# FFN input product in a fixed order on DVE and ACT, its weights one block ahead, its stores on POOL's queue

## The chip, the cores and the metric

The kernel runs on one core of a Trainium2 chip. The metric is device time in microseconds (us), the median of several runs. TensorE (PE) multiplies, VectorE (DVE), ScalarE (ACT) and GpSimd (POOL) work on tiles, SyncE (SP) and POOL issue transfers (DMA). Each engine has one queue of instructions and works through it in order; an instruction waits until what it reads is there, and holds all that stand behind it on its engine.

## The reference, cut to what matters

```python
for layer in range(2):                      # T = 1024 tokens, D_MODEL = 1024, D_FF = 2816
    hn = rmsnorm(h, norm_gains[layer, 0])
    mixed = fox_attention(hn, ...) if layer % 2 == 0 else hgrn2_recurrence(hn, ...)
    h = h + rmsnorm(mixed, norm_gains[layer, 1])
    hn = rmsnorm(h, norm_gains[layer, 2])
    h = h + rmsnorm(swiglu_ffn(hn, ffn_w_in[layer], ffn_w_out[layer]), norm_gains[layer, 3])

def swiglu_ffn(h, w_in, w_out):
    gate, up = jnp.split(jnp.einsum('bsd,df->bsf', h, w_in), 2, axis=-1)
    return jnp.einsum('bsf,fd->bsd', jax.nn.silu(gate) * up, w_out)
```

All of it is fp32.

## The kernel before

An fp32 product is three matmuls of a rounded type: each operand is split in a high part (a cast on ACT, L178) and a low part (a subtraction on DVE, L181), and hi·hi, hi·lo and lo·hi are summed in PSUM. `split` does both; the tiles are whi and wlo for weights, p1h and p1l to p7h and p7l for x.

The FFN input product multiplies 2 × 2 quadrants with seven products in place of eight: the quadrants of w_in (a11, a12, a21, a22) and of x (r11, r12, r21, r22) are first added and subtracted, then seven products p1 to p7 of 12 matmuls of 128 x 512 are made, then added into the results. `ffn_in` loops over 22 blocks of weight columns, gate and up in turn. From the fifth block on the order of products on PE is p1, p5, p4 of the block before, p2, p6, p3, p7. For the first four blocks p1 and p2 are computed ahead, from x operands that are ready early (`ffn_ahead`; `first` keeps copies of their p1).

`operands` loads a block's weights (wl, the two lower quadrants, L407; wst, the upper ones, L411, both on SP), forms the sums (L401) and splits them. It is called within the block, and the order in which DVE takes the sums, lo parts and results (`gate`, `up`: silu on ACT at L452, product with the up half at L459) is left to a scheduler that works from simulated times. Only the casts are chained among themselves (`queue`).

Of x, `Quadrants.put` writes a token tile's transposed columns (psx is their PSUM tile) into raw tiles; `Quadrants.sums` makes the sums for p5, p6, p3, p7 and p4 in two parts of 256 columns (four token tiles each). Both are called after the last tile of the mixer's output product. The last tile comes to it through `boundary`, which adds the mixer's output to h (`postnorm`, with rs from POOL), stores h (L333, SP), normalises it (`prenorm`, L281) and transposes it.

`out_sums` runs beside `ffn_in`: it loads rows of w_out (wrow, L538, SP), makes four sums of them (tsum, L544 to L548) and stores these (tw0a, tw0b, tw1a, tw1b, POOL's queue, L546, L549) for the FFN output product. The results of `ffn_in` go to DRAM as aT (L461, SP). `ffn_out` reads aT and tw back through ring tiles as and ws (L576, L597, SP), splits them, and hands its results (cx, cy, cu, cv; L628) to `boundary`, which in layer 2 stores the output out (L333, SP).

`hgrn_consts` makes the masks and bounds (lm, tb; L1005 to L1036) of the recurrence of layer 2; it is called after layer 1's `ffn_in`.

The lines that set pools and order:

```python
BUFS = dict(s=3, g=3, l=2, ws=2)
self.wst = pool("wst", 3)
with self.tc.issue_after(self.casts[queue].ins) if queue in self.casts else nullcontext():
```

Of the kernel before, what the change touches and what calls it, by code (L numbers as in the profile page):

```python
# [7 lines left out]
F32 = mybir.dt.float32  # L8
F32R = mybir.dt.float32r
# [41 lines left out]
BUFS = dict(s=3, g=3, l=2, ws=2)  # L51
# [7 lines left out]
DPOS = (1,)  # L59

# [13 lines left out]
class Quadrants:  # L74
# [9 lines left out]
    def __init__(self, pool, work):  # L84
        self.op, self.raw, self.work = {}, {}, work
        for n, tag in enumerate(self.PLACES):
            self.raw[self.NAMES[n % 4], n // 4] = work.tile([P, 4, 256], F32, name=self.NAMES[n % 4], tag=tag, bufs=BUFS[tag])
        self.take(pool, self.EARLY)
# [5 lines left out]
    def put(self, trunk, b, tt, ps):  # L94
# [3 lines left out]
        raw = self.raw[f"r{b + 1}{t + 1}", p // 2][:, :, p % 2 * P:(p % 2 + 1) * P]  # L98
# [5 lines left out]
    def sums(self, trunk, part):  # L104

        V = trunk.nc.vector
        r11, r22, r12, r21 = (self.raw[n, part] for n in self.NAMES)
        cs = slice(part * 256, (part + 1) * 256)
        split = lambda m, t, ks=slice(0, 4): trunk.split(*(x[:, ks, cs] for x in self.op[m]), t)
        n = 4 if part else 2  # L110
        for k in range(0, 4, n):
            ks = slice(k, k + n)
            if part:
                t = trunk.nrm.tile([P, n, 256], F32, name="rsum", tag="u", bufs=trunk.nb[1])
            else:
                t = self.work.tile([P, n, 256], F32, name="rsum", tag="ws", bufs=BUFS["ws"])
            V.tensor_tensor(out=t, in0=r12[:, ks], in1=r11[:, ks], op=ALU.subtract)
            split("p5", t, ks)
        V.tensor_tensor(out=r12, in0=r22, in1=r12, op=ALU.subtract)
        V.tensor_tensor(out=r11, in0=r12, in1=r11, op=ALU.add)  # L120
        split("p6", r11)
        split("p3", r22)
        split("p7", r12)
        V.tensor_tensor(out=r21, in0=r21, in1=r11, op=ALU.subtract)
        split("p4", r21)

class Trunk:
    def __init__(self, ctx, tc, a):
# [6 lines left out]
        self.sums_of, self.casts = {}, {}  # L135
        self.const = pool("const")
        self.wst = pool("wst", 3)
# [37 lines left out]
    def split(self, hi, lo, src, lo_engine=None, queue=None):  # L175

        with self.tc.issue_after(self.casts[queue].ins) if queue in self.casts else nullcontext():
            cast = self.nc.scalar.copy(out=hi, in_=src)  # L178
        if queue is not None:
            self.casts[queue] = cast  # L180
        (lo_engine or self.nc.vector).tensor_tensor(out=lo, in0=src, in1=hi.bitcast(F32), op=ALU.subtract)  # L181

    def unit(self, srcs, shape, keep=None):

        nc = self.nc
        with self.tc.high_priority(offset=self.ahead):
            st = self.wst.tile([P] + shape, F32, name="wst", tag="wst")
            for dst, src in srcs:
                nc.sync.dma_start(out=dst(st), in_=src)
# [86 lines left out]
    def prenorm(self, h, gB, xT, tt, keep=True, step=1):  # L276

        nc = self.nc
        rs = self.squares((h,))
# [1170 lines left out]
```

## Time and profile before

| | us |
|---|---|
| median of 3 runs (lowest, highest) | 2590.56 (2587.06, 2591.43) |
| profiled execution, its own time | 2588.12 |
| span of its profile | 2586.3 |
| PE busy | 2486.8 (96%) |
| FFN input product, layer 1 (638.12 to 1094.02) | 455.9, of which PE busy 438.4 |
| FFN input product, layer 2 (1894.73 to 2352.22) | 457.5, of which PE busy 439.3 |

The stages in order are: first norm, attention with its projections (to about 583), the attention's output product (to 638), FFN input and output of layer 1 (to about 1390), HGRN2 and its output product (to 1894), FFN of layer 2. The profile gives busy time of each engine in any stretch, a timeline with the idle time in front of an instruction and what ended it (in brackets), and a table of waits. PE's granted clock is 1.00 where it runs at its upper level.

### The profile page before, as it was taken

How to read it: one execution, taken by the hardware profiler on the slowest of the kernel's cores; microseconds unless marked ns; L12 is line 12 of the kernel's file. 1: busy time of each engine (PE TensorE's matmuls, PEld its weight loads, DVE VectorE, ACT ScalarE, POOL GpSimd, SP SyncE). 2: the span in 40 equal slices, each digit the busy share in tenths (PEclk: the TensorE clock that was granted, in tenths of full speed). 3: DMA queues.
4: the chain of work that ended last, by engine and by line, in shares of the span. 5: the costliest groups of instructions: out<-in, count | busy, mean ns of one | idle time of the engine just before them, and what ended most of it. 6: DMA issues, size and time to landing. Idle time of an engine off the chain costs nothing. (4 is left out here: it accounts for less than half of the span.)

```text
span 2586.3 us, 35183 instructions
## 1 busy us (share of the span) xinstructions
PE 2486.8 (96%) x12616; PEld 2079.6 (80%) x12616; DVE 1664.0 (64%) x2875; ACT 1105.0 (43%) x2128; POOL 432.7 (17%) x654
## 2 busy tenths in 40 slices
PE   6999999999898999999999999999999989999997
PEld 6898989878676888788879988887877778887885
DVE  5767676767766455476866585766575654455675
ACT  5556565655433333354542222223452333334443
POOL 4434343422000000000231111114200100000022
PEclk9999999999999999999999999999999999999998
DMA  4211111225478222384641211114534852226554
GB/s 123 47 34 37 41 35 34 62 86 169 115 227 265 87 73 83 93 297 135 220 135 38 74 46 55 48 58 139 175 107 155 275 169 84 78 70 226 185 181 166
DMA packets 302127, 305.43 MB, mean 118 GB/s; under 512 B 54648, under 2 KB 229752, under 8 KB 301952
## 3 DMA queue, kind: packets, MB, share of 16 engines
q1 hardware_dynamic: 292736, 275.91, 34.5%
q0 software_dynamic: 9216, 27.27, 3.2%
q8 instruction: 99, 1.62, 0.3%
q14 instruction: 76, 0.62, 0.1%
HBM read 228.67 MB, written 74.45 MB: 117 GB/s over the span
## 5 line engine op out<-in xcount | busy, mean ns | idle before, releaser
L157 PE MATMUL op<-whi,a 128*128 128x512 f32 x1232 | 384.4, 392 | 15.0 <-DVE cx L628 7.5
L178 ACT CAST whi<-wst 128x512 fp32r<-128x512 f32 x288 | 177.3, 619 | 410.7 <-PE m L157 201.7
L157 PEld LDWEIGHTS op<-whi,a 128*128 128x128 f32 x1232 | 232.2, 189 | 67.4 <-issue 8.3
L181 DVE TENSOR_TENSOR wlo<-wst,whi 128x512 fp32r<-128x512 f32 x240 | 168.2, 704 | 134.7 <-ACT whi L178 134.4
L157 PE MATMUL op<-wlo,a 128*128 128x512 f32 x616 | 241.0, 391 | 0.8 <-DVE wlo L181 0.8
L157 PE MATMUL pv<-whi,xTh 128*128 128x256 f32 x512 | 150.0, 293 | 4.4 <-DVE k L771 4.4
L157 PE MATMUL pv<-wlo,xTh 128*128 128x256 f32 x512 | 145.8, 285 | 0.0
L157 PE MATMUL pv<-whi,xTl 128*128 128x256 f32 x512 | 145.5, 284 | 0.0
L157 PEld LDWEIGHTS op<-wlo,a 128*128 128x128 f32 x616 | 116.2, 189 | 25.2 <-DVE wlo L181 1.4
L796 ACT ACTIVATE p<-p,mn 128x128 f32<-128x128 f32 (+7 forms) x128 | 99.2, 776 | 78.5 <-DVE mn L795 77.6
L181 DVE TENSOR_TENSOR pl<-pT,ph 128x512 fp32r<-128x512 f32 (+1 forms) x160 | 100.8, 633 | 47.5 <-ACT ph L178 44.5
L181 DVE TENSOR_TENSOR wlo<-wl,whi 128x512 fp32r<-128x512 f32 x88 | 60.4, 688 | 99.7 <-ACT whi L178 99.7
L795 DVE CUSTOM_DVE_ANT_0 p<-s,mask 128x128 f32<-128x128 f32 (+7 forms) x128 | 93.1, 755 | 37.3 <-PE s L157 36.5
L181 DVE TENSOR_TENSOR wlo<-ws,whi 128x512 fp32r<-128x512 f32 x154 | 104.9, 684 | 10.9 <-ACT whi L178 10.5
L157 PE MATMUL pqk<-xTh,whi 128*128 128x512 f32 x256 | 110.1, 430 | 0.0
L178 ACT CAST ph<-pT 128x512 fp32r<-128x512 f32 (+1 forms) x160 | 86.7, 544 | 50.7 <-PE pT L161 48.1
L178 ACT CAST whi<-ws 128x512 fp32r<-128x512 f32 x154 | 95.2, 619 | 22.3 <-DMA ws<-in_ffn_w_out_dram 7.6
L157 PEld LDWEIGHTS pv<-whi,xTh 128*128 128x128 f32 x512 | 97.9, 191 | 5.1 <-issue 4.6
L161 PE MATMUL pT<-ident,p 128*128 128x128 f32 x576 | 91.5, 277 | 10.6 <-DVE o L836 9.5
L157 PE MATMUL pqk<-xTl,whi 128*128 128x512 f32 x256 | 101.6, 397 | 0.0
L178 ACT CAST whi<-wl 128x512 fp32r<-128x512 f32 x88 | 54.5, 619 | 110.2 <-PE m L157 110.1
L157 PE MATMUL pqk<-xTh,wlo 128*128 128x512 f32 x256 | 101.3, 396 | 0.0
(355 smaller groups left out, 6867.0 us busy)
## 6 DMA issues: line engine op xcount, KB each, us to landing
as<-aT SPq DMA_DIRECT2D x132, 256.0 KB, 3.6
wst<-in_ffn_w_in_dram SPq DMA_DIRECT2D x104, 256.0 KB, 3.0
wl<-in_ffn_w_in_dram SPq DMA_DIRECT2D x44, 512.0 KB, 4.0
aT<-g SPq DMA_DIRECT2D x88, 256.0 KB, 3.0
wrow<-in_ffn_w_out_dram SPq DMA_DIRECT2D x44, 512.0 KB, 5.7
ws<-in_ffn_w_out_dram SPq DMA_DIRECT2D x66, 256.0 KB, 3.9
wst<-in_hgrn_w_in_dram SPq DMA_DIRECT2D x64, 256.0 KB, 2.8
h<-hb SPq DMA_DIRECT2D x24, 512.0 KB, 4.9
```

The lines of the kernel that those rows point to most:

```text
L157: i = self.last_mm = self.nc.tensor.matmul(*args, **kw)
L161: i = self.nc.tensor.transpose(**kw)
L178: cast = self.nc.scalar.copy(out=hi, in_=src)
L181: (lo_engine or self.nc.vector).tensor_tensor(out=lo, in0=src, in1=hi.bitcast(F32), op=ALU.subtract)
L795: nc.vector.tensor_tensor_reduce(out=p[:, 0:W], in0=s[:, 0:W], in1=self.mask[:, T - W:T], scale=1.0, scalar=BIG, op0=ALU.add, op1=ALU.min, ...
L796: nc.scalar.activation(out=p[:, 0:W], in_=p[:, 0:W], func=AF.Exp, bias=mn, scale=-1.0, accum_out=sm)
```

## The change

- `ordered` chains the DVE and the ACT instructions that are traced inside it, each engine's to the one before on that engine, so that both run in the order of the program. It holds the last tile's `boundary`, `ffn_start` and `ffn_in`, and the first product of `ffn_out`.
- `operands` returns a function `make`. The weights of block i+1 are made during block i: those of p1 after its p5, of p5 after p2, of p2 after p6, of p6 after p3, of p3 after p7, while p7 and p4 are made in their own block after p5. The lo part of an operand is issued only with the next cast (`parts`, `flush`).
- `ffn_start`, a generator, is run in steps (`fills`) between the steps of the last tile's `boundary`. It computes p1 and p2 of the first four blocks, copies p1, and makes the first weights and the last sums of x.
- In the first four blocks `first` is copied to PSUM and p6 added onto it by PE; before, DVE added it.
- `Quadrants.sums` works on a pair of token tiles, and only the last pair's sums are left after the last tile. The splits are in `cast`.
- `out_sums` loads wrow one step ahead, on POOL's queue. The stores of aT and of `boundary` go to POOL's queue too, except the output of token tiles 6 and 7. In `ffn_out` the loads of h are issued behind p3's last load.
- `hgrn_consts` is called in the attention's third head group.
- Buffers: l from 2 to 5, wst from 3 to 4. The program's `dynamic_dma_scratch_size` is 2048.

```diff
-BUFS = dict(s=3, g=3, l=2, ws=2)
+BUFS = dict(s=3, g=3, l=5, ws=2)
+PAIRS = {3: 1, 6: 2}
...
+    def ordered(self):
...
+        for i in traced[start:]:
+            if i.engine in queues:
+                if i.engine in before:
+                    self.tc.add_manual_dep(i, before[i.engine].name, mybir.DependencyInfo(mybir.DependencyClass.NoSync, mybir.DependencyReason.DATA), reason="ordered")
+                before[i.engine] = i
...
+    def parts(self, hi, lo, t):
+
+        self.nc.scalar.copy(out=hi, in_=t)
+        self.flush()
+        self.waiting.append(lambda: self.nc.vector.tensor_tensor(out=lo, in0=t, in1=hi.bitcast(F32), op=ALU.subtract))
...
+        def make(*names):
+            for m in names:
+                if m == "p5":
+                    s1.append(pool.tile([P, 4, P], F32, name="wsum", tag="ws", bufs=BUFS["ws"]))
+                    add(s1[0], a21, a22, ALU.add)
+                elif m == "p6":
+                    add(a11, s1[0], a11)
+                elif m == "p3":
+                    add(a12, a12, a11)
+                r[m] = self.ffn_parts({"p1": a11, "p5": s1 and s1[0], "p2": a12, "p6": a11, "p3": a12, "p7": a21, "p4": a22}[m], True)
+                if m == "p5":
+                    add(a21, a11, a21)
...
-            send = lambda: nc.sync.dma_start(out=rows, in_=r.rearrange("p (b x) -> p b x", b=2))
+            send = lambda: nc.gpsimd.dma_start(out=rows, in_=r.rearrange("p (b x) -> p b x", b=2))
...
+            self.product(c, r["p5"], x["p5"])
+            A.copy(out=p5, in_=c)
+            if before:
                 before()
-                product(a1, "p2", w["p2"], True)
+            if i >= n:
+                w[0]("p7", "p4")
+                make("p1")
+                self.product(a1, r["p2"], x["p2"], True)
                 done(0, 0, a1, None)
-                product(b, "p6", w["p6"], True)
+                make("p5")
+                self.product(b, r["p6"], x["p6"], True)
                 A.copy(out=u2, in_=b)
+                make("p2")
...
-                self.nc.sync.dma_start(out=t, in_=w_out[k * P:(k + 1) * P, :])
+                G.dma_start(out=t, in_=w_out[k * P:(k + 1) * P, :])
...
-        self.postnorm(y, gpost, h, own, lambda c: self.nc.sync.dma_start(out=hout[tt * P:(tt + 1) * P, c], in_=h[:, c]), [(self.nc.vector, self.nc.gpsimd)[e] for e in ENDP[xT is None]], ss)
+        self.postnorm(y, gpost, h, own, lambda c: (self.nc.sync if xT is None and tt > 5 else self.nc.gpsimd).dma_start(out=hout[tt * P:(tt + 1) * P, c], in_=h[:, c]), [(self.nc.vector, self.nc.gpsimd)[e] for e in ENDP[xT is None]], ss, fills)
...
+            if (h, j) == (2, 0):
+                self.hgrn_consts(self.const)
...
-        self.ffn_ahead(0, "p2", ahead)
-        xT.sums(self, 1)
-        aT, late = self.ffn_in(0, xT, fw[1], ahead)
+        with self.ordered():
+            fills = self.ffn_start(0, xT, fw[1], ahead)
+            next(fills)
+            bound1(ps, TT - 1, fills)
+            start = next(fills)
+            aT, late = self.ffn_in(0, xT, fw[1], ahead, start)
```

What the order of the instructions shows is given at three places. The first is DVE in layer 1, behind the normalisation of the last token tile (u): sums of x (r11, r12, r22, rsum), their lo parts, and weights of the first blocks. Before:

```order
L181 TENSOR_TENSOR p3l_7506<-r22_6885,p3h_7505 128x4x256
L119 TENSOR_TENSOR r12_6886<-r22_6885,r12_6886 128x1024
L181 TENSOR_TENSOR wlo_7700<-wst_7683,whi_7699 128x512
L181 TENSOR_TENSOR wlo_7704<-wl_7680,whi_7703 128x512
L181 TENSOR_TENSOR p5l_7502<-rsum_7554,p5h_7501 128x4x256
L401 TENSOR_TENSOR wst_7773<-wst_7773,wst_7772 128x512
L120 TENSOR_TENSOR r11_6884<-r12_6886,r11_6884 128x1024
L181 TENSOR_TENSOR p7l_7508<-r12_6886,p7h_7507 128x4x256
L459 TENSOR_TENSOR g_7712<-g_7712,m_7571 128x512
L181 TENSOR_TENSOR wlo_7708<-wl_7680,whi_7707 128x512
L124 TENSOR_TENSOR r21_6887<-r21_6887,r11_6884 128x1024
L181 TENSOR_TENSOR wlo_7779<-wsum_7776,whi_7778 128x512
```

After, from the last pair's sums on:

```order
L116 TENSOR_TENSOR r11_6950<-r12_6952,r11_6950 128x512
L426 TENSOR_TENSOR p5l_7550<-rsum_7480,p5h_7549 128x4x128
L426 TENSOR_TENSOR p6l_7552<-r11_6950,p6h_7551 128x4x128
L426 TENSOR_TENSOR p3l_7554<-r22_6951,p3h_7553 128x4x128
L442 TENSOR_TENSOR wst_7617<-wst_7617,wst_7616 128x512
L426 TENSOR_TENSOR p3l_7554<-r22_6951,p3h_7553 128x4x128
L426 TENSOR_TENSOR wlo_7766<-wst_7617,whi_7765 128x512
L426 TENSOR_TENSOR p7l_7556<-r12_6952,p7h_7555 128x4x128 x2
L560 TENSOR_TENSOR g_7819<-g_7819,m_7560 128x512
L118 TENSOR_TENSOR r21_6953<-r21_6953,r11_6950 128x512
L426 TENSOR_TENSOR wlo_7774<-wl_7614,whi_7773 128x512
L426 TENSOR_TENSOR p4l_7558<-r21_6953,p4h_7557 128x4x128 x2
```

The first gate product (g) stands ahead of a sum of x and of two lo parts of block 0's weights (wlo_7774 is p7's) in the program's order, and the pieces of x are half as large.

The second is the queue that loads in the FFN input product of layer 1. SP before:

```order
L407 DMA wl_7874<-in_ffn_w_in_dram 128x8x128
L411 DMA wst_7877<-in_ffn_w_in_dram 128x4x128
L411 DMA wst_7980<-in_ffn_w_in_dram 128x4x128
L407 DMA wl_7978<-in_ffn_w_in_dram 128x8x128
L461 DMA aT0_7569<-g_7906 256x1x256
L411 DMA wst_7981<-in_ffn_w_in_dram 128x4x128
L538 DMA wrow_8219<-in_ffn_w_out_dram 128x1024
L411 DMA wst_8084<-in_ffn_w_in_dram 128x4x128
L461 DMA aT0_7569<-g_7712 256x1x256
L407 DMA wl_8082<-in_ffn_w_in_dram 128x8x128
L461 DMA aT0_7569<-g_7767 256x1x256 x2
```

SP after, some blocks on:

```order
L447 DMA wst_8944<-in_ffn_w_in_dram 128x4x128
L447 DMA wst_8945<-in_ffn_w_in_dram 128x4x128
L444 DMA wl_9387<-in_ffn_w_in_dram 128x8x128
L447 DMA wst_9092<-in_ffn_w_in_dram 128x4x128
L447 DMA wst_9093<-in_ffn_w_in_dram 128x4x128
L444 DMA wl_9536<-in_ffn_w_in_dram 128x8x128
```

and POOL after, in the same stage:

```order
L562 DMA aT0_7777<-g_8269 256x1x256 x2
L562 DMA aT0_7777<-g_8326 256x1x256
L665 DMA tw0a_7778<-tsum_8483 128x1024
L649 DMA wrow_8491<-in_ffn_w_out_dram 128x1024
L666 DMA tw0b_7779<-tsum_8484 128x1024
L649 DMA wrow_8492<-in_ffn_w_out_dram 128x1024
L562 DMA aT0_7777<-g_8326 256x1x256
L665 DMA tw0a_7778<-tsum_8632 128x1024
L649 DMA wrow_8640<-in_ffn_w_out_dram 128x1024
L666 DMA tw0b_7779<-tsum_8633 128x1024
```

The stores of aT and the loads of wrow have left SP's queue, where they stood between the loads of weights, for POOL's, where they stand between the stores of tsum.

The third is the end of the last FFN output product, layer 2. SP before:

```order
L333 DMA out_0_dram<-h_22804 128x512 x2
L597 DMA ws_23052<-tw1b_18265 128x512
L576 DMA as_23070<-aT1_18158 128x512
L597 DMA ws_23075<-tw1b_18265 128x512
L576 DMA as_23093<-aT1_18158 128x512
L327 DMA h_23291<-hb2_81 128x1024
L333 DMA out_0_dram<-h_22870 128x512 x2
L333 DMA out_0_dram<-h_22936 128x512 x2
L597 DMA ws_23098<-tw1b_18265 128x512
L576 DMA as_23116<-aT1_18158 128x512
```

SP after:

```order
L695 DMA as_23060<-aT1_18306 128x512
L716 DMA ws_23065<-tw1b_18308 128x512
L695 DMA as_23083<-aT1_18306 128x512
L351 DMA h_23279<-hb2_81 128x1024
L716 DMA ws_23088<-tw1b_18308 128x512
L695 DMA as_23106<-aT1_18306 128x512
L716 DMA ws_23111<-tw1b_18308 128x512
L695 DMA as_23129<-aT1_18306 128x512
```

POOL after, at the same place, where rs_23281 is that of the token tile h_23279 loaded in the rows above:

```order
L285 TENSOR_TENSOR rs_22888<-rs_22888,mhalf_77 128x1
L357 DMA out_0_dram<-h_22817 128x512 x2
L285 TENSOR_TENSOR rs_22954<-rs_22954,mhalf_77 128x1
L357 DMA out_0_dram<-h_22883 128x512 x2
L357 DMA out_0_dram<-h_22949 128x512 x2
L282 TENSOR_SCALAR rs_23281<-ss_23044 128x1
L341 TENSOR_TENSOR cu_21312<-cu_21312,gB_21292 128x512
L285 TENSOR_TENSOR rs_23281<-rs_23281,mhalf_77 128x1
```

The stores of out_0_dram stood ahead of the last ring loads (ws, as) on SP, and stand now on POOL ahead of the norm's rs.

## Rows read from the trace of the kernel before

**Rows 1.** The page, section 1: busy us (share of span), instructions.
```profile
PE 2486.8 (96%) x12616; PEld 2079.6 (80%) x12616; DVE 1664.0 (64%) x2875; ACT 1105.0 (43%) x2128; POOL 432.7 (17%) x654
```

**Rows 2.** Busy time by stretch: length, PE, PEld, DVE, ACT, POOL, PEclk, DMA share, GB/s.
```profile
583.00:638.00 55.00, 55.00 (x262) 44.77 (x261) 38.00 (x45) 28.87 (x56) 12.81 (x24) 1.00 0.53 170
638.12:1094.02 455.90, 438.37 (x1865) 349.97 (x1863) 259.67 (x402) 167.95 (x286) 14.60 (x28) 0.99 0.43 135
1894.73:2352.22 457.49, 439.32 (x1859) 351.05 (x1857) 257.63 (x390) 164.75 (x282) 14.15 (x26) 0.99 0.42 134
2540.00:2586.30 46.30, 33.09 (x132) 26.17 (x132) 21.90 (x34) 12.85 (x29) 10.07 (x12) 0.87 0.32 114
```

**Rows 3.** PE timeline, start, length, line, operation: two starts of p4; transposes.
```profile
652.65 1.03 PE L161 MATMUL psx<-ident,u 128*128 128x128 f32 x8
...
2099.67 0.39 PE L157 MATMUL m<-p4h,whi 128*128 128x512 f32 x1
...
2119.21 0.39 PE L157 MATMUL m<-p4h,whi 128*128 128x512 f32 x1
```

**Rows 4.** PE timeline of the FFN input products; in brackets idle before, releaser.
```profile
658.35 0.50 PE L157 MATMUL m<-p2h,whi 128*128 128x512 f32 x1 [1.93 <-ACT p L477]
...
661.71 0.63 PE L157 MATMUL m<-p2l,whi 128*128 128x512 f32 x1
662.13 0.63 PE L157 MATMUL m<-p2h,wlo 128*128 128x512 f32 x1
...
1090.96 0.50 PE L157 MATMUL m<-p4h,whi 128*128 128x512 f32 x1 [0.78 <-DVE s L401]
...
1914.16 0.50 PE L157 MATMUL m<-p2h,whi 128*128 128x512 f32 x1 [1.93 <-ACT p L477]
...
2077.54 0.80 PE L157 MATMUL m<-p4h,whi 128*128 128x512 f32 x1 [6.55 <-ACT m L495]
...
2349.14 0.50 PE L157 MATMUL m<-p4h,whi 128*128 128x512 f32 x1 [0.78 <-DVE s L401]
```

**Rows 5.** Waits of DVE and of SP's queue: us in total, times, longest.
```profile
DVE wsum L401 <- DMA wl<-in_ffn_w_in_dram: 45.0, 35, 3.9
...
DVE tsum L544 <- DMA wrow<-in_ffn_w_out_dram: 34.0, 16, 4.2
...
SPq L461 <- DVE g L459: 183.2, 56, 6.6
```

**Rows 6.** The chain of waits, 2000 to 2080: start, length, what.
```profile
2014.54 0.53 POOL tw1a L546
...
2066.79 6.30 DMA tw1a<-tsum
```

**Rows 7.** The page, section 5: weight casts and lo parts, busy, mean ns.
```profile
L181 DVE TENSOR_TENSOR wlo<-wl,whi 128x512 fp32r<-128x512 f32 x88 | 60.4, 688 | 99.7 <-ACT whi L178 99.7
...
L178 ACT CAST whi<-wl 128x512 fp32r<-128x512 f32 x88 | 54.5, 619 | 110.2 <-PE m L157 110.1
```

**Rows 8.** Issues of transfers: count, KB each, median us to landing.
```profile
wl<-in_ffn_w_in_dram SPq DMA_DIRECT2D x44, 512.0 KB, 4.0
aT<-g SPq DMA_DIRECT2D x88, 256.0 KB, 3.0
...
tw0b<-tsum POOLq DMA_DIRECT2D x11, 512.0 KB, 6.8
```

**Rows 9.** Timeline at the end: SP's queue, then PE.
```profile
2525.96 3.46 SPq L333 DMA_DIRECT2D out_dram<-h  x4
...
2542.38 0.76 PE L157 MATMUL op<-whi,a 128*128 128x512 f32 x1 [7.55 <-DVE cx L628]
```

**Rows 10.** Timeline: DVE beside POOL, a mask operation, PE in the attention.
```profile
2509.22 1.77 DVE L322 SCALAR_TENSOR_TENSOR h<-cy,rs,h 128x512 f32<-128x512 f32 x1
...
1100.32 0.23 DVE L1031 TENSOR_SCALAR lmf<-lmf 128x128 f32<-128x128 f32 x1
...
64.89 0.36 PE L157 MATMUL pv<-whi,xTh 128*128 128x256 f32 x1 [4.40 <-DVE k L771]
```

More of the change, by code (lines that the diff above doesn't have):

```diff
@@ L173, in po, with split @@
         return self.ps.tile([P, D], F32, name=name, tag="po", bufs=2)
[L175 to L180, printed above, removed]
+    @contextmanager
+    def ordered(self):
+        traced = self.nc.cur_bb.bb.instructions
+        last = traced[-1]
+        yield
+        start = next(k for k in reversed(range(len(traced))) if traced[k] is last) + 1
+        queues = [q.engine for q in (self.nc.vector, self.nc.scalar)]
+        before = {}
+        for i in traced[start:]:
[3 more added lines that the diff above has]
+                before[i.engine] = i
+    def split(self, hi, lo, src, lo_engine=None):
+        self.nc.scalar.copy(out=hi, in_=src)
         (lo_engine or self.nc.vector).tensor_tensor(out=lo, in0=src, in1=hi.bitcast(F32), op=ALU.subtract)
@@ L304, in postnorm_first, with postnorm @@
         return ss
-    def postnorm(self, y, gB, h, own, store, engines, ss=None):
+    def postnorm(self, y, gB, h, own, store, engines, ss=None, fills=None):
         nc = self.nc
@@ L380, with ffn_load, ffn_parts @@
     FIRST = (0, DFF, 2 * P, DFF + 2 * P)
+    def ffn_load(self, layer, m, n):
+        kh = Quadrants.EARLY.index(m)
+        t = self.wst.tile([P, 4, P], F32, name="wst", tag="wst")
+        c0 = self.FIRST[n]
+        self.nc.sync.dma_start(out=t, in_=self.a["ffn_w_in"][layer][kh * HALF:(kh + 1) * HALF, c0:c0 + P].rearrange("(k p) c -> p k c", p=P))
+        return t
+    def ffn_parts(self, t, wait=False):
+        hi, lo = (self.wun.tile([P, 4, P], F32R, name=f"w{s}", tag=f"w{s}") for s in ("hi", "lo"))
+        self.parts(hi, lo, t)
+        if not wait:
+            self.flush()
+        return hi, lo
@@ L384, in ffn_ahead @@
         w_in = self.a["ffn_w_in"][layer]
[L385 to L392 removed]
+        c0 = i % 2 * DFF + i // 2 * 2 * P
@@ L396, in ffn_in @@
+    def ffn_in(self, layer, xT, pool, ahead, start):
         nc = self.nc
@@ L1002, in hgrn_consts @@
         self.gn = pool.tile([P, 1], F32, name="gn")
-        with nc.allow_non_contiguous_dma(reason="3 rows of bounds and 128 gains"), self.tc.issue_after(self.last_first.ins):
+        with nc.allow_non_contiguous_dma(reason="3 rows of bounds and 128 gains"), self.tc.issue_after(self.last_unit.ins):
             for r in range(3):
@@ L1269, in run @@
             bound1(y, tt)
+        list(xT.sums(self, 0))
         ov = oT.rearrange("(k p) t -> p k t", p=P)
@@ L1408, in run @@
         xT2.take(ry[1])
-        xT2.sums(self, 0)
-        self.ffn_ahead(1, "p2", ahead)
-        xT2.sums(self, 1)
-        aT, late = self.ffn_in(1, xT2, fw[1], ahead)
+        with self.ordered():
+            fills = self.ffn_start(1, xT2, fw[1], ahead)
+            next(fills)
+            bound(ps, TT - 1, fills)
+            start = next(fills)
+            aT, late = self.ffn_in(1, xT2, fw[1], ahead, start)
         g7 = self.gain(gains[1, 3])
```

289 lines of the change are left out of this document (175 added, 114 removed).

## The prediction, made before the changed kernel ran

> **What bounds the kernel now.** I read the engine busy line first: TensorE is busy 2486.8 of 2586.3 us and VectorE 64% [rows 1]. The matmul list is not shortened by this change, so only the 99.5 us in which TensorE is idle, and the time in which it runs at the lower clock, can be won. Next I read the busy time by stage, to see where that time lies. The two FFN input products, cut at their first and last matmul, hold 455.9 − 438.4 = 17.5 us and 457.5 − 439.3 = 18.2 us of it, and the last 46.3 us of the program hold 13.2 us at a mean granted clock of 0.87 [rows 2]. These are the places the change touches.
>
> Then I measured what these stages would take without a stall. One block in the steady part takes 2119.21 − 2099.67 = 19.54 us, p4 to p4, and there are 22 blocks: 429.9 us. The stages are longer, and of that only the transposes of late token tiles are work, 1.03 us for the eight of a tile [rows 3] (two tiles in layer 1, one in layer 2). So layer 1 loses 455.9 − 429.9 − 2 = **24 us** and layer 2 457.5 − 429.9 − 1 = **26.6 us**, 50.6 together.
>
> The TensorE timeline of the two stages names 11 gaps in layer 1, from 658.35 to 1090.96, and 10 in layer 2, from 1914.16 to 2349.14; the largest is 6.55 us [rows 4]. Their idle time is 35 us. The other 15 us are matmuls that follow a gap: at 661.71 they start 0.42 us apart [rows 4], while 12 of them take a seventh of 19.54 us, 0.23 each, in the steady block. That is the lower of the two clock levels, 1.2 in place of 2.4 GHz. All in, one gap costs 50.6 / 21 = **2.4 us**. All but the last lie in the first eight or nine of the 22 blocks; after 2077.54 the next is the one at 2349.14 [rows 4], and layer 1 is alike.
>
> What ends the gaps is read from their releasers and from the wait lists. ACT and DVE release them (copies at L495, the gate product L459), but these were held back themselves: DVE waits 45.0 us in all for the load `wl`, 34.0 us for `wrow`, and SP's queue, which holds those loads, stands 183.2 us behind stores of aT that wait for DVE [rows 5]. The chain of waits ahead of the largest gap shows the same from the other side: a store of tw1a takes 6.30 us, a tsum waits for it, and the result sums and the ACT copy that TensorE needs come after that tsum [rows 6].
>
> **The change part by part.**
>
> *Weights one block ahead, DVE and ACT in a fixed order.* Work per block stays: seven casts of 0.62 and seven lo parts of 0.69 us [rows 7], four weight sums and the result sums of about 0.69. For DVE, 7 lo parts, 4 sums and 4 result operations are 15 × 0.69 = 10.3 us, and four tsum operations, in the blocks that carry them, 2.8 more: 10 to 13 us of 19.5. So no engine is full, and order decides. What now needs a load by the time of its own block needs it a block earlier, but the loads move ahead as well (pools l from 2 to 5 buffers, wst from 3 to 4); a `wl` takes 4.0 us [rows 8] against a block of 19.5, so I cost the loads at nothing. If that cover is gone, each costs the 3.9 us of the largest wait on `wl` [rows 5].
>
> In-order waits are the price. I followed the new DVE and ACT order against the TensorE order through the first blocks, with these durations. In block 0 the lo part that p7 needs stands behind the gate product, which waits for an ACT table load and a silu: about 1.1 us. In block 1 p5 waits about 1.4 us for its lo part. The last p4 keeps its 0.78 us [rows 4], because nothing follows it. That is 3 gaps where 11 and 10 stood. At 2.4 us each this is 7.2 us; by their own lengths (1.1 + 1.4 + 0.8 = 3.3) and a lower clock in the first two it is about 5. I take 6 per layer: **layer 1 gains 18, layer 2 20.6, together −38.6 us**. Bounds: all 50.6, if nothing of it remains; half of it, 25, if as many gaps remain as in one of the two layers now.
>
> *Sums of x per pair of tiles.* Three of four pairs move ahead of the last output tile, into a stretch where TensorE has 55 us of work in 55 us and DVE 38 [rows 2], so they hide. It is this that empties DVE between the last tile and p5; the gain is in the sum above. If the cover is gone, one pair is four sums and five casts at 0.6 to 0.7, some 6 us.
>
> *Stores and wrow on POOL's queue.* SP's queue then carries only wl and wst in these stages, so no load stands behind a DVE-dependent store. POOL is busy 14.6 of 456 us there [rows 2], and one issue costs it 0.53 us [rows 6]; 88 stores of aT and 44 wrow are 70 us of 917, beside other work. A 512 KB store from that queue lands after 6.8 us where an aT store on SP's takes 3.0 [rows 8]; with three g tiles and one used in a block of 19.5 us, 3.8 more hide. I cost this at nothing, up to the rival below.
>
> The Trainium skill, "DMA: Bandwidth & Descriptors", section "Issuing engines are not separate DMA queues", says that a second issuing engine saves only the issue time, as all transfers share the same 16 DMA engines. By that rule this part would give nothing but 0.5 us per store; the trace differs, since what is saved here is the in-order wait of 183.2 us [rows 5].
>
> *The tail.* Before the last product SP holds four out stores that wait for DVE, 3.46 us from 2525.96, ahead of loads ws and as; what is made from these ends the 7.55 us gap at 2542.38 [rows 9]. With the stores of tiles up to 5 on POOL, the loads start up to 3.5 us sooner. But the wait has other parts (the loads themselves, the casts and lo parts behind it, the sums at L628). I take **−4** (the gap 3.5 shorter, and less of the slow matmuls behind it), bounds 0 and −9.5 (the whole gap, and 2 us of matmuls at the lower clock, about the cost by gap above). At the very end POOL's queue now holds stores of tiles 4 and 5 before the rs of tile 7 on which the last store depends: two to four issues of 0.53 [rows 6], **+1.3**, bounds +1 and +2.
>
> *hgrn_consts in the attention.* 37 mask operations of 0.23 [rows 10] and 11 small ones are some 10 us of DVE work, moved from the start of the FFN output product, where TensorE did not wait for them, into the second head group of attention, where DVE is short (gap of 4.40 at 64.89 [rows 10]). Bounds 0 and +6 (a bit over half of them exposed); I take **+1.5**, nearer the low end, since the 4.40 us are the one gap over 1 us that waits for DVE there.
>
> *Sum.* −38.6 − 4 + 1.3 + 1.5 = −39.8. The profiled execution took 2588.12 us (its span is 2586.3; 1.8 lie outside), so it would take 2548.3. The median of the runs is 2590.56, 2.4 above it; from there the forecast is **2550.8 us**, 1.5% faster.
>
> **The rivals.**
>
> *Half the stalls stay.* An in-order engine that waits for TensorE holds everything behind it, and the first four blocks have the least slack. If about half of the 21 gaps remain, 25 us are won, no gain comes at the tail, and the consts cost 3: 2590.6 − 25 + 1.3 + 3 = **2570**. For it: the gaps now lie in just these blocks. Against: the order as followed shows three, not ten.
>
> *The new order stalls in every block (slower).* The pattern that I found in block 0, a lo part which TensorE needs, queued on DVE behind a result operation that itself waits for TensorE or ACT, could recur in each block: 44 × 2.4 = 106 us in place of 50.6, so 2590.6 + 55 = **2646**. It decides from 21 stalls on, about one in every second block. Against: in the order the weights of block i+1 stand between the results of block i, with a block to spare.
>
> *POOL becomes the slow link.* If POOL's issues wait for DVE, a store lands late, g tiles are missed, and silu and the gate product with them. The trace shows the two engines disturbing each other: the same DVE operation takes 1.77 us at 2509.22 beside POOL work in place of some 0.7. If each of the 132 moved issues cost TensorE a third of that extra, 1.0 us, some 45 us would be lost and the gain with it: 2550.8 + 45 = **2596**, no change or a little worse. Against: three g tiles and two wrow ahead are slack of tens of us.
>
> The Trainium skill, "SBUF — State Buffer", section "Who interferes with whom", states the rule behind this: descriptors of DMAs from POOL's queue are written by GpSimd, and it is locked out of the port pair which it shares with DVE while DVE holds it. By that rule the stores would sit till the DVE operation's end; no row here shows a store from this queue held in that way.
>
> **How the numbers follow.** My forecast 0.60, half the stalls 0.24, POOL 0.08, slower in every block 0.08. The range leaves out the last two (0.16): its low end is all 50.6 and the whole tail won with free consts, 2590.6 − 50.6 − 9.5 + 1 = 2531.5; the high end is half the stalls with the consts at +6 and stores at +2, 2590.6 − 25 + 8 = 2573.6, say 2574. A measurement of this kernel can tell some 0.2% (5 us) from no change. Faster by more: 0.60 + 0.24 and a part of the POOL case, 0.86; within: 0.05; slower by more: 0.09.
>
> **What would show it.** Right: in the FFN input stages no `wl` or `wrow` wait on DVE, no aT store on SP, three TensorE gaps per layer under 1.5 us, layer stages of about 438 us; the gap at the start of the last product near 4 us. Wrong: rows of TensorE waiting for `wlo` or `g` in blocks past the fourth; POOL's queue waiting long before its aT stores; attention stretch longer than before by more than 3 us.

## The result and the profile after

The changed kernel takes 2553.26 us (median of 4 runs, 2552.73 to 2553.61). Before, beside it, took 2590.99 us. The ratio is 0.9854, with a 95% interval of 0.9837 to 0.9871: 1.5% faster. The forecast was 2550.8 us in a range of 2531.5 to 2574. The experiments ran on three other occasions, each with the kernel before beside them: e1, e2, e3 and e9 on chip 1 (before: 2584.1 us), e4 to e7 on chip 8 (2583.8), e8 and e10 to e12 on chip 15 (2581.0). The changed kernel itself was run again on chip 15 alone: 2552.8 us, a ratio of 0.9885 (0.9867 to 0.9903). The change is faster there too, but the kernel before is 10 us faster there than in the first measurement and the changed one is not. Why is open; no profile of before was taken there.

The page of the changed kernel, section 1, and its busy time by stretch (length, PE, PEld, DVE, ACT, POOL, PEclk, DMA share, GB/s), each FFN input stage cut from the last matmul of the mixer's output product to the first of the FFN output product, then a stretch of steady blocks:

```profile
PE 2472.9 (97%) x12616; PEld 2074.8 (81%) x12616; DVE 1661.9 (65%) x2889; ACT 1104.6 (43%) x2142; POOL 544.0 (21%) x832
...
642.38:1079.91 437.53, 433.35 (x1867) 348.61 (x1866) 255.29 (x395) 170.66 (x296) 55.87 (x92) 1.00 0.47 145
1877.38:2314.93 437.55, 433.36 (x1867) 348.60 (x1866) 255.17 (x395) 169.83 (x295) 55.95 (x92) 1.00 0.45 142
700.00:1070.00 370.00, 370.00 (x1591) 298.59 (x1590) 207.30 (x326) 130.71 (x228) 48.39 (x80) 1.00 0.43 136
```

The first two answer [rows 2]. Cut in the same way, the stages before took 456.95 and 459.13 us; now both take 437.5. From 700 to 1070 TensorE is busy in all of the 370 us, at a granted clock of 1.00. What waits remain are seen in its timeline, which answers [rows 4] and [rows 9] (start, length, operation; in brackets idle before and releaser):

```profile
676.72 0.50 PE L162 MATMUL m<-p7h,wlo 128*128 128x512 f32 x1 [1.25 <-DVE wlo L426]
677.05 0.40 PE L162 MATMUL m<-p7h,whi 128*128 128x512 f32 x1
...
681.06 0.50 PE L162 MATMUL m<-p5h,wlo 128*128 128x512 f32 x1 [1.15 <-DVE wlo L426]
...
684.06 0.50 PE L162 MATMUL m<-p4h,whi 128*128 128x512 f32 x1 [0.41 <-DVE g L541]
...
2311.16 0.50 PE L162 MATMUL m<-p4h,whi 128*128 128x512 f32 x1 [0.78 <-DVE s L541]
...
2312.49 0.50 PE L162 MATMUL m<-p4h,wlo 128*128 128x512 f32 x1 [0.60 <-DVE wlo L426]
...
2506.97 0.76 PE L162 MATMUL op<-whi,a 128*128 128x512 f32 x1 [9.01 <-DVE cx L747]
```

Five short gaps in a layer, all in block 0, block 1 and at the end, stand where 11 and 10 stood. The gap at the start of the last product grew from 7.55 to 9.01 us. DVE's table of waits has no line for `wl` or `wrow` any more. The stores of aT now wait on POOL (table of waits; then the page's issues of transfers, and the issue time on POOL in ns, min, median, max):

```profile
POOL aT L562 <- DVE g L560: 538.7, 87, 21.6
...
aT<-g POOLq DMA_DIRECT2D x88, 256.0 KB, 2.7
...
L562 POOL DMA_DIRECT2D aT<-g x88: 672/679/699, 675.8 to 2316.2; - x88
```

POOL waits 539 us for them. Behind them stand the loads of wrow and the stores of tsum, and DVE has no wait for wrow, so nothing that TensorE needs is held.

For all kernels, the starts of the same matmuls in the profiles give the length of each stage (us):

| kernel | to the FFN input, layer 1 | FFN input 1 | FFN output 1, up to the recurrence's q | FFN input 2 | FFN output 2 | span |
|---|---|---|---|---|---|---|
| before | 637.7 | 456.9 | 226.5 | 459.1 | 224.1 | 2586.3 |
| after | 642.4 | 437.5 | 226.9 | 437.5 | 226.2 | 2551.3 |
| after, chip 15 (e12) | 642.4 | 437.5 | 226.3 | 437.6 | 227.7 | 2551.8 |
| e1, aT and wrow on SP | 642.7 | 440.5 | 230.1 | 440.1 | 231.0 | 2564.9 |
| e2, no fixed order | 643.1 | 448.3 | 227.9 | 447.3 | 230.2 | 2576.8 |
| e3, before, aT and wrow on POOL | 638.7 | 454.4 | 233.4 | 453.2 | 228.7 | 2591.0 |
| e4, consts back | 640.8 | 437.5 | 228.5 | 437.5 | 227.3 | 2552.1 |
| e5, out stores on SP | 641.8 | 437.5 | 226.8 | 437.5 | 227.3 | 2551.0 |
| e6, cx sums first | 640.5 | 437.5 | 226.9 | 437.5 | 223.6 | 2546.0 |
| e7, p7's lo part first | 641.0 | 437.1 | 226.7 | 437.1 | 227.6 | 2550.0 |
| e8, fewer buffers | 642.7 | 449.0 | 227.0 | 449.5 | 229.4 | 2581.1 |
| e10, e6 and e7 | 643.7 | 438.0 | 227.6 | 438.0 | 224.9 | 2552.4 |
| e11, and h loads late | 641.3 | 437.1 | 226.1 | 438.0 | 220.8 | 2543.6 |

With the fixed order and the changed queues and buffers, the FFN input stage takes 437.5 us in every profile, to 0.1 us; with e7's step added (e7, e10, e11) it takes 437.1 to 438.0. The first column differs by some 3 us among kernels that do the same work there; 1 to 2 us of it have arisen in the first 65 us of the program.

### The profile page after: what moved, and what is told of

The parts are those of the page before. It is cut to its first block, busy times and chain, and to the rows that moved or that the text cites. A ratio compares the mean times of both kernels' runs of the same rounds, so it can differ in the third digit from the quotient of the medians.

```text
span 2551.3 us, 35050 instructions
## 1 busy us (share of the span) xinstructions
PE 2472.9 (97%) x12616; PEld 2074.8 (81%) x12616; DVE 1661.9 (65%) x2889; ACT 1104.6 (43%) x2142; POOL 544.0 (21%) x832
## 3 DMA queue, kind: packets, MB, share of 16 engines
q0 software_dynamic: 27168, 89.15, 10.4%
## 4 chain that ended last, share of the span: by engine, by line
PE 86%; DVE 5%; issue 3%; DMA 2%; ACT 2%; POOL 1%; SPq 0%; POOLq 0%; DVEq 0%; ACTq 0%
PE m L162 33%; PE op L162 11%; PE pv L162 7%; PE pqk L162 6%; PE po L162 6%; PE phf L162 3%; PE phq L162 3%; PE phg L162 3%; PE s L162 3%; PE ot L162 3%; PE pT L166 2%; PE lv L162 2%; PE pe L162 2%; DMA as<-aT 1%; PE psx L166 1%
## 5 line engine op out<-in xcount | busy, mean ns | idle before, releaser
L562 POOL DMA_DIRECT2D aT<-g x88 | 59.8, 680 | 542.0 <-DVE g L560 538.7
L426 DVE TENSOR_TENSOR wlo<-wst,whi 128x512 fp32r<-128x512 f32 x176 | 120.1, 685 | 15.4 <-ACT whi L424 15.1
L198 DVE TENSOR_TENSOR pl<-pT,ph 128x512 fp32r<-128x512 f32 (+1 forms) x160 | 100.6, 633 | 43.0 <-ACT ph L197 39.8
```

What stands on the lines that cost most here:

```text
L426: self.waiting.append(lambda: self.nc.vector.tensor_tensor(out=lo, in0=t, in1=hi.bitcast(F32), op=ALU.subtract))
L562: send = lambda: nc.gpsimd.dma_start(out=rows, in_=r.rearrange("p (b x) -> p b x", b=2))
```

## The experiments

Three explanations of the gain stood against each other: weights made a block ahead (A), loads no longer behind stores on SP's queue (B), and the fixed order of DVE and ACT (C). The differences below are taken from the changed kernel's 2552.8 us. For e8, e10 and e11 that is the same chip. For the others it is not, so the ratio to the kernel before on their own chip is given where it matters; e5 and e7 on chip 8, which differ little from the changed kernel, took 2552.7 and 2552.4 us.

**The queue, undone (e1).**

```diff
-            send = lambda: nc.gpsimd.dma_start(out=rows, ...)
+            send = lambda: nc.sync.dma_start(out=rows, ...)
...
-                G.dma_start(out=t, in_=w_out[k * P:(k + 1) * P, :])
+                self.nc.sync.dma_start(out=t, in_=w_out[k * P:(k + 1) * P, :])
```

> The changed kernel with the stores of aT and the loads of wrow put back on SP's queue; everything else stays. If the gain comes from weights made a block ahead (A), the loads have about one block, 19.5 us, of slack behind the stores, and the time rises by no more than 4 us, to 2553 to 2557. If it comes from the queue (B), the waits for wl and wrow return with their gaps, and most of the 40 us won in the two FFN input stages go: 2575 to 2590.

Measured: 2566.25 us, 13 more (ratio to before beside it 0.9928, 0.9909 to 0.9947); neither range holds it. The FFN input product keeps the gaps of the changed kernel and no other. What it lost stands behind it, at the start of the FFN output product. PE's timeline of e1, then SP's queue there:

```profile
1083.18 1.47 PE L162 MATMUL op<-whi,a 128*128 128x512 f32 x4 [2.83 <-ACT whi L197]
1118.57 0.80 PE L162 MATMUL op<-whi,a 128*128 128x512 f32 x1 [3.56 <-ACT cu L759]
...
1068.43 9.21 SPq L562 DMA_DIRECT2D aT<-g  x3
1077.70 1.57 SPq L695 DMA_DIRECT2D a<-aT  x3
```

Three stores of aT hold SP's queue for 9.21 us ahead of the loads of a and ws for the next product. So the queue matters, but for the hand-over: in a block there is slack for the store, at the hand-over there is none. About 6 of the 13 us are in the two FFN input columns (which hold this first wait), 7 in the output columns.

**The order, undone (e2).**

```diff
             if i.engine in queues:
-                if i.engine in before:
+                if False:
```

> The changed kernel without the chain that fixes the order of DVE and ACT; the pipeline, the sums per pair and the queues stay, and the order of DVE and ACT is again the scheduler's. If the fixed order is what removes the gaps (C), ten or so gaps of 2.4 us return in each layer: 2580 to 2600. If weights a block ahead suffice in any order (A), the time stays within 6 us of the changed kernel: 2550 to 2559.

Measured: 2576.55 us, 23.8 more (ratio to before beside it 0.9977, 0.9967 to 0.9988). That is nearer to C, though below its range; A alone falls. The FFN input stages lose 10.8 and 9.8 us. Not ten gaps came back but fewer and longer ones: in layer 1 2.71, 1.43, 3.67 and 2.28 us in place of the changed kernel's 1.25, 1.15 and 0.41. PE and DVE of e2 at p5 of block 0, layer 1:

```profile
670.22 0.50 PE L162 MATMUL m<-p5l,whi 128*128 128x512 f32 x1 [2.71 <-DVE p5l L426]
...
666.47 0.68 DVE L442 TENSOR_TENSOR wsum<-wl 128x512 f32<-128x512 f32 x1
...
669.48 0.68 DVE L426 TENSOR_TENSOR p5l<-rsum,p5h 128x512 fp32r<-128x512 f32 x1
```

DVE works without a break, but on weight sums and on lo parts of p3 and p4, which TensorE needs later, while TensorE waits 2.71 us for p5's part of x, which comes 3 us later in DVE's queue; p6 follows with 1.43 and 3.67. Having work ready ahead gives a scheduler more to do in the wrong order.

**The queue alone, on the kernel before (e3).** Its aT stores and wrow loads are issued by POOL, as in the changed kernel.

```diff
-            send = lambda: nc.sync.dma_start(out=rows, ...)
+            send = lambda: nc.gpsimd.dma_start(out=rows, ...)
...
-                self.nc.sync.dma_start(out=t, in_=w_out[k * P:(k + 1) * P, :])
+                self.nc.gpsimd.dma_start(out=t, in_=w_out[k * P:(k + 1) * P, :])
```

> The kernel before with one part of the change alone: stores of aT and loads of wrow on POOL's queue. If the queue is the cause (B), 20 to 40 us are won: 2550 to 2570. If the pipeline is (A), the waits for wl shrink but the gaps of the first blocks, which wait for casts and sums in DVE's and ACT's queues, stay: 2583 to 2592.

Measured: 2592.66 us against 2584.09 of before beside it (ratio 1.0038, 1.0025 to 1.0050): 0.4% slower, 0.7 us above the range given for A. B falls as the cause. The FFN input stages win 2.5 and 5.9 us and the output stages give back 6.9 and 4.6. DVE's table of waits of e3, then SP's queue in e3 and, last, in the kernel before:

```profile
DVE tsum L544 <- DMA wrow<-in_ffn_w_out_dram: 47.6, 22, 8.9
...
DVE wsum L401 <- DMA wl<-in_ffn_w_in_dram: 37.8, 32, 5.1
...
SPq L411 <- DVE wlo L181: 585.4, 88, 18.9
...
SPq L411 <- DVE wlo L181: 303.6, 83, 8.8
```

The waits for wl and wrow of [rows 5] are still there, 38 and 48 us. SP's loads of wst no longer stand behind stores, but they wait 585 us, in place of 304, for a lo part that still reads their buffer: the in-order wait has become a wait for a free buffer.

**The order alone, on the kernel before (e9).** DVE and ACT follow the program's order within its FFN input product, with the weights made inside their own block.

```diff
...
-        aT, late = self.ffn_in(0, xT, fw[1], ahead)
+        with self.ordered():
+            aT, late = self.ffn_in(0, xT, fw[1], ahead)
...
```

> The kernel before with the other part alone: DVE and ACT held to the program's order within the FFN input product, weights still made inside their own block. This tests the price of the rival that forecast a stall in every block: the lo part of a block's first product then stands behind the results of the block before. If an in-order queue stalls TensorE whenever that happens (the rival's mechanism), there is a gap of 1 to 3 us in each of the 44 blocks and the time is 2640 to 2720. If slack hides it, the time stays at 2580 to 2600.

Measured: 2839.31 us, 255 more than before (2584.09). This is the slower rival's mechanism, and its price is far above the 2.4 us a block that I gave it. PE's timeline of e9, rows with a gap in two blocks; DVE ahead of the first of them; and the busy time of a steady stretch:

```profile
850.79 0.79 PE L157 MATMUL m<-p1h,wlo 128*128 128x512 f32 x1 [4.30 <-DVE wlo L196]
...
859.39 0.50 PE L157 MATMUL m<-p4h,whi 128*128 128x512 f32 x1 [1.02 <-ACT m L510]
...
875.57 0.50 PE L157 MATMUL m<-p1h,whi 128*128 128x512 f32 x1 [1.95 <-ACT whi L193]
...
877.65 0.80 PE L157 MATMUL m<-p1h,wlo 128*128 128x512 f32 x1 [1.29 <-DVE wlo L196]
...
905.45 0.80 PE L157 MATMUL m<-p1h,wlo 128*128 128x512 f32 x1 [4.30 <-DVE wlo L196]
...
846.79 0.69 DVE L474 TENSOR_TENSOR g<-g,s 128x512 f32<-128x512 f32 x1
...
850.05 0.68 DVE L196 TENSOR_TENSOR wlo<-wst,whi 128x512 fp32r<-128x512 f32 x1
...
850.00:1050.00 200.00, 165.60 (x610) 126.71 (x610) 92.19 (x144) 52.31 (x92) 7.97 (x15) 0.87 0.42 134
```

Two blocks take 905.45 − 850.79 = 54.66 us, 27.3 each in place of 19.54: 7.8 us a block. There are two or three gaps in each, and the granted clock averages 0.87. The lo part that TensorE waits for stands on DVE behind a result product (g), which itself waits for a product of TensorE, and behind four tsum operations between the two rows. So order without a block's lead is far worse than no order, lead without order (e2) keeps half of what the FFN input stages gained, and with both they gain all of it. The sums of x per pair of tiles and p6 added onto `first` by PE are in e2 and in the changed kernel alike, and no run took them out by themselves.

**Fewer buffers (e8).**

```diff
-BUFS = dict(s=3, g=3, l=5, ws=2)
+BUFS = dict(s=3, g=3, l=3, ws=2)
...
-        self.wst = pool("wst", 4)
+        self.wst = pool("wst", 3)
```

> The changed kernel with fewer buffers for weights: wst 3 as before the change, l 3 in place of 5. If the deeper pools are needed for weights a block ahead, loads come late and DVE waits for wl in each block: TensorE gaps in the steady blocks and 10 to 40 us more, 2563 to 2593. If the pipeline has slack for a load of 4 to 5 us in a block of 19.5, the FFN input stages keep 437.5 us and the time stays within 3 us of the changed kernel.

Measured: 2582.39 us, 29.6 more; the whole gain on this chip is gone (ratio to before 1.0002, 0.9991 to 1.0013). But not for the reason that the expectation names. Busy time, PE timeline and waits of SP's queue of e8:

```profile
720.00:1075.00 355.00, 355.00 (x1527) 286.57 (x1526) 198.28 (x312) 125.03 (x218) 47.03 (x78) 1.00 0.44 139
...
665.79 0.50 PE L162 MATMUL m<-p2h,whi 128*128 128x512 f32 x1 [1.58 <-ACT whi L424]
...
1091.75 2.07 PE L162 MATMUL op<-whi,a 128*128 128x512 f32 x4 [7.16 <-ACT whi L197]
...
SPq L716 <- DVE wlo L426: 10.3, 1, 10.3
```

The steady blocks have no wait: TensorE is busy in 355.00 of 355.00 us. The cost is at the two ends of the stage. At its start, with the wait of 1.58 us at p2, the two layers lose 4.2 and 4.5 us up to p7 of block 0. At the hand-over they lose 7.3 and 7.4, with a gap of 7.16 in layer 1, where the first loads of the FFN output's ring wait 10.3 us on SP for a lo part (wlo) of the last block. That is 15 of the 29.6 us at the hand-overs and 9 at the starts; the rest lies outside the stage. By this trace the smaller pools let the ring's tiles lie where the last block's weights still were, so the deeper pools pay as space that comes free earlier. That reading is from the trace alone; the placement was not varied by itself.

**The masks back (e4).**

```diff
-            if (h, j) == (2, 0):
-                self.hgrn_consts(self.const)
...
         g3, g4 = self.gain(gains[0, 3]), self.gain(gains[1, 0])
+        self.hgrn_consts(self.const)
```

> The changed kernel with hgrn_consts called behind layer 1's FFN input product again. If its DVE work costs what the attention lost up to 201 us (4.0 us there, +4.7 up to the last attention output tile), the time falls by 4 to 5 us, to 2548.5 to 2549.5, unless the FFN output product pays for it, which in the kernel before it did not. If the attention's loss has another cause, the time stays within 1 us of 2553.3.

Measured: 2556.49 us (2553.86 to 2562.3), not faster; its profiled run is the fastest of the four. PE's timeline of the attention, at the same two places, in the changed kernel and then in e4, and a third place in e4:

```profile
64.81 0.55 PE L162 MATMUL pv<-whi,xTh 128*128 128x256 f32 x1 [4.39 <-DVE k L893]
...
201.11 0.66 PE L166 MATMUL pT<-ident,p 128*128 128x128 f32 x4 [0.86 <-DVE o L958]
```
```profile
63.49 0.55 PE L162 MATMUL pv<-whi,xTh 128*128 128x256 f32 x1 [4.38 <-DVE k L893]
...
197.54 0.65 PE L166 MATMUL pT<-ident,p 128*128 128x128 f32 x4 [0.85 <-DVE o L958]
...
445.81 0.66 PE L166 MATMUL pT<-ident,p 128*128 128x128 f32 x4 [3.58 <-DVE o L958]
```

From the first place to the second it is 136.3 us with the masks and 134.05 without: 2.25 us. At the third place 2.7 us are lost again, in a gap of 3.58 where the changed kernel has 0.87, and the FFN output of layer 1, where the masks then are, takes 1.6 to 2.2 us more. So the masks cost some 2 us in either place, and the 4 to 5 us that I expected back were mostly not theirs.

**The tail: where the output is stored (e5).** All output stores go by SP.

> The changed kernel with all stores of the output on SP's queue, as before the change. If the gap at the start of the last product (now 9.0 us, before 7.55) grew because stores and ring loads now run at once, it falls back to about 7.5 us and the time to about 2551.5. If the order of the stores does not matter to that gap, it stays at 9 and only the end, 1 us of POOL issues, changes: 2552 to 2553.

Measured: 2552.66 us, the gap 8.95 and the end 0.2 us shorter. The queue of these stores does not set the gap; the second reading holds. Nor do the loads start sooner where POOL stores. SP's first load of p4's weights in the kernel before and in the changed one, then a row of SP's waits in the latter, from 2470 to 2512:

```profile
2521.57 0.33 SPq L597 DMA_DIRECT2D ws<-tw1b  x1
...
2486.25 0.32 SPq L716 DMA_DIRECT2D ws<-tw1b  x1
...
SPq L716 <- DVE wlo L198: 10.5, 8, 4.5
```

The load is issued 2521.57 − 2352.60 = 169.0 us into the stage before and 2486.25 − 2314.93 = 171.3 us after, in both as soon as DVE has made a lo part that still read its buffer.

**The tail: DVE's order (e6).** The lo parts of p4's second and later steps are tied behind the last cx sum.

```diff
-        (lo_engine or self.nc.vector).tensor_tensor(out=lo, ...)
+        with self.tc.issue_after(self.hold.ins) if self.hold else nullcontext():
+            (lo_engine or self.nc.vector).tensor_tensor(out=lo, ...)
...
-        product("p4", ps, onto=True, j1=n - KEEP)
+        product("p4", ps, onto=True, j1=n - KEEP, hold=last)
```

> The changed kernel with one order fixed at the start of the last product (p4 of the FFN output): the lo parts of p4's second and later steps come behind the four sums cx on DVE; before, the sums stood behind the lo parts of p4's first five steps, which wait for their loads. If the gap of 9.0 us is an in-order wait on DVE (D1), it falls to 2 to 3 us and the time by 6 to 8, to 2545 to 2547. If it is the transfers' throughput (D2; DMA share 1.04 in the gap), TensorE waits for the same loads a step later and the time stays within 2 us of 2553.3.

Measured: 2548.52 us, 4.3 less, and 4.1 less than e5 on the same chip. Timeline of e6, PE, then ACT and DVE ahead of the second gap:

```profile
2496.84 0.47 PE L162 MATMUL op<-whi,a 128*128 128x512 f32 x1 [0.84 <-DVE cx L749]
...
2504.78 0.80 PE L162 MATMUL op<-wlo,a 128*128 128x512 f32 x1 [4.48 <-DVE wlo L199]
...
2493.93 0.62 ACT L197 CAST whi<-ws 128x512 fp32r<-128x512 f32 x1 [6.12 <-DMA ws<-tw1b]
...
2501.56 0.62 ACT L197 CAST whi<-ws 128x512 fp32r<-128x512 f32 x1 [2.37 <-DMA ws<-tw1b]
...
2502.83 0.69 DVE L325 TENSOR_TENSOR cx<-cx,gB 128x512 f32<-128x512 f32 x1 [4.94 <-ACT junk L292]
...
2504.04 0.69 DVE L199 TENSOR_TENSOR wlo<-ws,whi 128x512 fp32r<-128x512 f32 x1
```

The wait for the sums is down from 9.01 to 0.84 us, so D1 holds for that part. The 4.48 us that stay come one step later (p4 has eleven steps, each with its own loads), and the trace shows an order there too. TensorE waits for the second step's wlo, made at 2504.04. Three wlo follow the sums, at 2504.04, 2505.24 and 2506.45, and ACT's last three casts of weights before them are at 2493.93, 2496.91 and 2501.56. So the second step's weights were cast at 2493.93, and their load had landed 10 us before they were used. Their lo part stands on DVE behind the product of cx with its gain (L325), which waits 4.94 us for ACT's first sum of squares of cx (junk). On ACT this stands behind the cast for the fourth step, which waits 2.37 us for its load. A load is at the end of that chain, but not one that the second step needs. No run changed this order, so what it would win is not shown.

**Block 0's lo part (e7).**

```diff
         w0[0]("p7")
+        self.flush()
```

> The changed kernel with the lo part for p7 of block 0 issued on DVE ahead of the gate product that it stood behind. If the step of the prediction holds, the gap of 1.25 us at p7 of block 0 disappears in each layer, and perhaps the one of 1.15 us behind it, for 1.5 to 5 us in all: 2548 to 2552. If the lo part is late for another reason (its cast on ACT), the gap stays and the time is 2553.

Measured: 2552.44 us, not to be told from the changed kernel's time; each FFN input stage takes 437.1 in place of 437.5. The 1.25 us gap is gone, and a new one stands next to it, in e7's timeline:

```profile
677.31 0.50 PE L162 MATMUL m<-p5h,whi 128*128 128x512 f32 x1 [0.95 <-ACT whi L424]
679.19 0.51 PE L162 MATMUL m<-p5h,wlo 128*128 128x512 f32 x1 [1.15 <-DVE wlo L426]
```

The place was as the prediction named it, but behind it the weights of block 1's p5 were as late, so freeing one lo part moved the wait.

**Both (e10), and h loaded late (e11).** e10 is e6 with e7; e11 adds, for the last layer:

```diff
         ops = [(j, left("p4", j), right("p4", j)) for j in range(n - KEEP, n)]
+        if layer:
+            self.rows_after = loads[-1]
```

> The changed kernel with both orders: p7's lo part of block 0 ahead of the gate product, and the cx sums ahead of the lo parts of p4's later steps. If the two are independent (4.7 us and 0.8 us alone), 2547 to 2549. If the order before the last product depends on more than that, as much as 2 us of it is lost: 2549 to 2551.

> As the one before, and in the last layer the loads of h for the last four token tiles, 512 KB each, are issued behind p4's last ring load; before they came behind p3's. If what is left of the gap at the last product (0.84 + 4.48 us with the order fixed) is transfers that share the DMA engines (D2 for the rest), taking 2 MB out of that stretch wins 3 to 4 us: 2543 to 2546. If it is DVE or ACT, nothing changes: 2547 to 2549. Should h then come late for the last tiles, the end waits up to 4 us longer.

Measured: e10 2549.25 us (2547.03 to 2554.22, which does not tell its two readings apart), and e11 2544.62 us (2542.88 to 2545.35; ratio to before 0.9852, 0.9832 to 0.9873, where the changed kernel has 0.9885 beside it). Timeline of e11, PE and DVE; then busy time by stretch, two of e11 and one of e6:

```profile
2504.51 0.50 PE L162 MATMUL op<-wlo,a 128*128 128x512 f32 x1 [2.89 <-DVE wlo L199]
...
2502.56 0.69 DVE L325 TENSOR_TENSOR cx<-cx,gB 128x512 f32<-128x512 f32 x1 [3.35 <-ACT junk L292]
...
2500.00:2505.00 5.00, 2.11 (x10) 1.43 (x9) 2.44 (x5) 3.50 (x10) 0.00 (x0) 1.00 0.15 54
2505.00:2510.00 5.00, 5.00 (x24) 4.08 (x23) 5.00 (x10) 1.87 (x3) 0.00 (x0) 1.00 0.89 292
...
2505.00:2510.00 5.00, 5.00 (x14) 3.90 (x15) 5.00 (x9) 2.25 (x6) 0.00 (x0) 0.56 0.90 281
```

With 2 MB of loads out of the stretch the second gap falls from 4.48 (e6) to 2.89, and FFN output 2 from 223.6 to 220.8; e10's profile, with 5.47 and 224.9, is of its slowest run. Two things can be read from the traces. The fourth step's load takes 4.4 us from its issue to its cast in place of 5.3, as it would where transfers share; the place of the h loads in SP's queue, where they waited 10.4 us in e6, did not hold it, since it is issued 184 us into the stage in both. And TensorE's granted clock, 0.56 behind e6's gap, is 1.00 behind this one. What is left of the gap is not transfers: the DMA share is 0.15 from 2500 to 2505, and the chain through L325 and junk stands there as in e6. e11 is 8.2 us faster than the changed kernel and the fastest measured here.

**The changed kernel on chip 15 (e12).** 

> The changed kernel itself, run beside the next three, so that they are compared on one chip. All theories: 2551 to 2555.

 Measured: 2552.8 us.

## Why the prediction was right, and where it was not

- *The two FFN input stages, −18 and −20.6.* Measured −19.4 and −21.6 (456.9 and 459.1 to 437.5). The order as followed by hand gave 1.1, 1.4 and 0.78 us for three gaps in a layer; the trace has 1.25, 1.15 and 0.78, plus two of 0.41 and 0.60. What remains over 22 steady blocks and the transposes of two tiles is 437.5 − 429.9 − 2 = 5.6 us, 4.2 of it these gaps; I took 6.
- *Loads and buffers at nothing.* Right for the steady blocks, in which e8 shows no wait even with the smaller pools. Wrong as a statement on the pools: without them 29.6 us are lost, at the start of the stage and, most of it, at the hand-over. I costed l and wst as cover for loads, and did not ask what lies in that space next.
- *Stores and wrow on POOL at nothing.* Right for the blocks, but the reason I gave for part of the gain, the 183.2 us of [rows 5], was mostly not a loss: moving the queue alone makes the kernel before slower (e3). Undoing it costs 13 us (e1), at the hand-over that I did not look at. The rule cited from the Trainium skill, "DMA: Bandwidth & Descriptors", section "Issuing engines are not separate DMA queues", therefore fits e3 (no gain) and not e1, where what stands behind a waiting store is what costs.
- *POOL as the slow link.* It did not happen. Stores on POOL's queue land after 2.7 us, where SP's took 3.0 [rows 8], and an issue takes 0.68 us. The longest of the 88 issues took 0.70 us, beside a DVE that is busy in 255 of 437.5 us. The Trainium skill, "SBUF — State Buffer", section "Who interferes with whom", which the prediction drew on, leaves `tensor_tensor` out of the operations that hold such transfers up. 393 of DVE's 395 operations in the stage are of that kind, so the trace agrees with the page, and the rival was weaker than I made it.
- *The tail, −4.* This step failed, by sign: +1.5 in the gap, +2.1 in the stage. I read the four stores on SP's queue as what held the loads [rows 9]. They were not: with the stores back on SP the gap is 8.95 us, and with them on POOL the loads start no sooner, since they wait for DVE (e5). The releaser in the row was the key. It says cx, and cx stood in DVE's queue behind lo parts of five steps whose loads were under way. That order was worth 4 us (e6). What stayed was again an order, through ACT, and in part transfers (e11).
- *The end, +1.3.* From the start of the last matmul of the program to the end it took 9.7 us before and takes 10.2: +0.5.
- *The masks, +1.5.* They cost 2.25 us in the attention (e4), near the forecast. But the stretch ahead of the FFN input is 4.7 us longer, and it is so with or without them: from the gap at 64.8 on it takes 577.6 us in the changed kernel, 577.3 in e4 and 572.8 before. The changed kernel has gaps of 2.95 and 2.42 us at 516.9 and 532.5, e4 of 1.42 and 2.42, where before had none over 0.8 there. I had no term for that, and which part of the change causes it was not tried.
- *The sum.* Profile against profile: −19.4 − 21.6 + 2.1 + 0.5 + 4.7, and −1.4 between FFN input 1 and 2, are the −35.0 of the spans. I had −39.8. The larger gain in the FFN (2.4 us) hid a part of a miss of 6 us at the tail and 3 in the attention. By medians the change is −37.7, since before's profiled run lay 2.9 us under its median and after's lies at its own. That half of the miss of 4.8 us does not show in the forecast of 2550.8 is luck: I had added 2.4 us for the first of these two distances, and there is no such distance after the change.
- *The rivals.* "Half the stalls stay" (2570) is near what e2 shows without the fixed order: 2576.6. "A stall in every block" is not what the changed kernel does; e9 does it, with 7.8 us a block and not 2.4, since a block then has two or three gaps, and the lower clock goes on between them.

## What to carry to other kernels

Work made one block ahead and a fixed order of the engines gave half of the stage's gain or did harm apart (−20 us of 41 in e2, +255 us in e9), and all of it together; test them as one. Where stages hand over, ask what the next stage's first loads stand behind, in their queue and in the space they take: both cost more here (13 us in e1, some 15 in e8) than anything in the steady blocks. When a wait names its releaser, look at what stands ahead of that releaser on its own engine before blaming the queue beside it, and follow that to the next engine: in e6 the second gap led from TensorE over DVE and ACT to a load that TensorE did not need yet.

## What the runs showed of the hardware

I had put 2.4 us all-in on a gap. The gaps of 1.25 and 1.15 us cost their own length: the matmul behind the one at 676.72 starts 0.33 us later, the next ones 0.23, and the stage's granted clock is 1.00. Behind the gap of 1.93 us in [rows 4] matmuls started 0.42 us apart, and in e9, with gaps of 4.30, 1.02, 1.95 and 1.29 us in two blocks, the clock averaged 0.87. The length of a gap does not settle it either. Busy time of the kernel before in layer 1, around the gap of 1.93 us and around one of 2.51 (at 702.30):

```profile
657.00:665.00 8.00, 6.65 (x22) 5.30 (x23) 8.00 (x10) 4.84 (x6) 0.00 (x0) 0.79 0.24 68
...
697.00:712.00 15.00, 12.49 (x54) 9.73 (x54) 7.55 (x22) 6.76 (x11) 0.00 (x0) 1.00 0.48 106
```

The gap of 2.51 us left the clock at 1.00, the shorter one did not. So a mean price over 21 gaps is no price of one, and what a gap costs beyond its length is to be read from the granted clock behind it.
